# Output weights of an attention layer gated and split in an earlier stage, and the merge of its patterns begun two slots later

## The chip, the cores and the metric

The kernel runs on one core of one Trainium2 chip. The metric is the device time of the whole program in microseconds (us). Less is better. TensorE is called PE here, VectorE DVE, ScalarE ACT, GpSimd POOL, SyncE SP.

## The reference, cut to what matters

A trunk of two layers over a sequence of 1024 rows of 1024 features, in float32. Layer 0 mixes by a gated MLP (gMLP), layer 1 by dilated attention; each is followed by a squared-ReLU MLP of 4096 hidden features. Every sub-layer is modulated by a conditioning vector: `h = x * (1 + scale) + shift; x = LayerNorm(alpha * x + gate * f(h))`. The change concerns the attention of layer 1 and its output weights:

```python
def mixer_b(h, w_qkv, w_out, slopes):
    B, S, _ = h.shape
    qkv = (h @ w_qkv).reshape(B, S, N_PAT, 3, B_HEADS, B_HEAD_DIM)
    outs, lses = [], []
    for g, (window, dilation) in enumerate(B_PATTERNS):   # (128,1), (512,4), (2048,16)
        o, lse = dilated_branch(qkv[:, :, g, 0], qkv[:, :, g, 1], qkv[:, :, g, 2],
                                window, dilation, slopes)
        outs.append(o); lses.append(lse)
    wts = jax.nn.softmax(jnp.stack(lses, axis=0), axis=0)[..., None]
    o = jnp.sum(wts * jnp.stack(outs, axis=0), axis=0)
    return o.reshape(B, S, B_HEADS * B_HEAD_DIM).astype(h.dtype) @ w_out
```

There are 16 heads of 64, three patterns (dilation 1, 4 and 16), and a softmax over the patterns' log-sums merges their outputs. The gate, a row of 1024 numbers, multiplies the columns of `o @ w_out`; the kernel multiplies it into the columns of `w_out` instead.

## The kernel before

Float32 operands are split into a high and a low part (`hi` is a cast by ACT, `lo` is the remainder by DVE; lines L102 and L103 of a helper `split`), and each product is three matmuls: hi x hi, hi x lo, lo x hi. The MLPs and the projections of the attention go by a seven-product scheme on 2 x 2 blocks of 512.

In order of time the program is: layer 0's mixer and MLP; **the values stage** (function `values`); **the attention** (function `attention`), with the projection of q and k of the dilated patterns woven in; the output projection; the second MLP (`mlp(3, ...)`).

The values stage runs over `V_STEPS`, five sets of seven products `p`: v of pattern 2, of pattern 1, of pattern 0, then q and k of pattern 0 (the undilated one, `g == 0`). A product takes four steps `m`, each with 12 matmuls into `psv` (L1257). Weights are loaded raw (`vraw`, two products ahead, method `load` of `RightForms`), some into tiles of a tag `res` and others of other tags (helper `raw_tile`), and split one product ahead into `vrhi`, `vrlo`. `evict` combines, splits and stores results: v, q and k go to DRAM over POOL's queue.

The attention takes 24 groups, three patterns of each of eight pairs of heads `hp`; a group owns eight slots, and a slot has ordered lists of pieces of work, put there with `at(slot, half)`. A group's pieces are scores, a softmax pass (ACT and DVE), transposes, `halve` (tiles pT into `pThi`, `pTlo`), `weighted` (matmuls `pv<-pThi,v` and `pv<-pTlo,v`, L1527) and `gather` (ACT and DVE add the halves of `pv` into `oT`, L1536 and L1537). When a pair's three patterns are there, `merge(hp, oTs)` reads their log-sums, forms weights, writes them to `w_dram`, loads them spread over partitions into `bc` (L1611 and others) and does twelve steps on DVE: scale `oT` by `bc` (L1623), add (L1627), cut into high and low. For pairs 0 to 6 these steps are put at slots from `base + 9` on, where `base` is the first slot after the pair's last group; pair 7's are called by hand in `go_on`.

The output projection sums 8 units `k` (one pair of heads each, 128 rows of `w_out`) in five calls of `accumulate`: a (units 0 to 3, first half of the rows, tile `psoa`), b (0 and 1, second half, `psob`), c (2 and 3, `psoc`), d (4 to 7, first half, `psod`) and e (4 to 7, second half, `psoe`). a and b run inside the last groups' slots, c and d after them in `go_on`, and e is a callback at the entry of the second MLP. A unit's weights are made by `staged_unit`: the raw 512 KB load (L1708), the product with the gate row (L1712), and the split into `wo_hi` and `wo_lo`, each at a slot given relative to the last group. Raw tiles have the tag `raw` (2 buffers), hi and lo tiles the tags `whi` and `wlo` (4 buffers each). The tag `raw` also serves the raw weights `up` of the MLPs (L754).

Within each engine the order is the program's only where `keep_in_program_order` asks for it; elsewhere a scheduler orders by its own model. Each engine works its queue in order, and SP issues the loads in order, each once its tile is free.

Of the kernel before, what the change touches and what calls it, by code (L numbers as in the profile page):

```python
# [10 lines left out]
F32 = mybir.dt.float32  # L11
F32R = mybir.dt.float32r
AF = mybir.ActivationFunctionType
ALU = mybir.AluOpType
# [3 lines left out]
P = 128  # L18
S = 1024
D = 1024  # L20
NT = S // P
KD = D // P
HALF = 512
D_FF = 4096
N_HEADS = 16
N_PAIRS = N_HEADS // 2
# [9 lines left out]
def trunk(ctx: ExitStack, tc: tile.TileContext, x, c, ada_w, ada_b, ln_g, ln_b, a_w_in, a_b_in,  # L36
# [3 lines left out]
    nc = tc.nc  # L40
    V, A, G, T = nc.vector, nc.scalar, nc.gpsimd, nc.tensor

    def pool(stack, name, bufs, **kw):
        return stack.enter_context(tc.tile_pool(name=name, bufs=bufs, reuse_waits="tile", **kw))
# [5 lines left out]
    wts = pool(ctx, "wts", 4)  # L50
    work = pool(ctx, "work", 2)
    dram = pool(ctx, "dram", 1, space=DRAM)
# [44 lines left out]
    def bank(kind, name):  # L97
        return ps[kind].tile([P, HALF], F32, name=name, tag=kind)

    def split(hi, lo, src, hi_engine=A, lo_engine=V):  # L100

        first = A.copy(hi, src) if hi_engine is A else hi_engine.tensor_copy(hi, src)  # L102
        return first, lo_engine.tensor_tensor(lo, src, hi, op=ALU.subtract)  # L103
# [4 lines left out]
    gate_dram = dram.tile([4, D], F32, name="gate_dram")  # L108
# [93 lines left out]
    def run(gen):  # L202
        for _ in gen:
            pass
# [867 lines left out]
    v_dram = [dram.tile([S, N_PAIRS, 4 * HEAD], F32, name=f"v_{g}") for g in range(3)]  # L1072

    qk_dram = dram.tile([N_PAIRS, 2, P, 2, S], F32, name="qk_0")

    class RightForms:
        BLOCK = {1: (0, 0), 2: (1, 0), 5: (0, 1), 6: (1, 1), 7: (0, 1), 4: (1, 0)}
# [53 lines left out]
    def values(before, right, ahead):  # L1131
        run(ahead)
        form = before.form
        name = {1: "L11", 2: "L12", 5: "S1", 6: "S2", 7: "S3", 4: "L22", 3: "S4"}
        with ExitStack() as ph:
# [12 lines left out]
            def x_tile(nm):  # L1148
                return xp.tile([P, HALF], F32, name=nm, tag="x")
# [12 lines left out]
            def place(f, k, src):  # L1162
                split(form[f][:, 0, k, :], form[f][:, 1, k, :], src)
# [48 lines left out]
            stream = second()  # L1212
            sums, parts = {}, {}

            def evict(g, X, p, m):
                acc = sums["pb" if p in (2, 5, 3) else "pa", m][:]
                if p in (1, 5, 6):
                    t = parts[p, m] = x_tile(f"vpart_{g}_{X}_{p}_{m}")
                    A.copy(t[:], acc)
                    return  # L1220
                if p != 4:
                    t = parts.pop(({2: 1, 7: 5, 3: 6}[p], m))
                    V.tensor_tensor(t[:], acc, t[:], op=ALU.add)
                    acc = t[:]
                half, dh = {2: (1, 0), 3: (1, 1), 4: (0, 0), 7: (0, 1)}[p]
                if X < 2:
                    t = parted.tile([P, 2, HALF], F32R, name=f"qs_{X}_{p}_{m}", tag="vs")
                    split(t[:, 0], t[:, 1], acc)
                    nc.gpsimd.dma_start(qk_dram[4 * dh + m, X, :, :, half * HALF : (half + 1) * HALF], t[:].bitcast(F32))
                    return  # L1230
                v = parted.tile([P, 4, 4, HEAD], F32R, name=f"vs_{g}_{p}_{m}", tag="vs")
                split(v[:, :, 0:4:3, :], v[:, :, 1:3, :], acc.rearrange("p (h e c) -> p h e c", e=2, c=HEAD))
                i = 4 * half + m
                nc.gpsimd.dma_start(v_dram[g][i * P : (i + 1) * P, 4 * dh : 4 * dh + 4, :],
                                  v[:].rearrange("p h f c -> p h (f c)").bitcast(F32))

            for n, (g, X, p) in enumerate(V_STEPS):
                while name[p] not in built:
                    next(stream)
                for m in range(4):  # L1240
                    if m % 2 == 0 and n + 1 < len(V_STEPS):
                        right.prepare(*V_STEPS[n + 1], m // 2)
                    if m % 2 and n + 2 < len(V_STEPS):
                        right.load(*V_STEPS[n + 2], m // 2)
                    if p in (1, 2, 5):
                        kind = "pa" if p == 1 else "pbx" if m > 1 and n > 1 else "pb"
                        sums["pa" if p == 1 else "pb", m] = bank(kind, f"psv{p}_{g}_{X}_{m}")
                    acc = sums["pb" if p in (2, 5, 3) else "pa", m][:]
                    left = form[name[p]]
                    for kp in range(2):  # L1250
                        r = right.ready[g, X, p, kp]
                        for k in range(2):
                            for a, b in TERMS:
                                rows, cols_ = left[:, a, 2 * kp + k], r[b][:, k]
                                if X < 2:
                                    rows, cols_ = r[a][:, k], left[:, b, 2 * kp + k]
                                T.matmul(acc, rows[:, m * P : (m + 1) * P], cols_,  # L1257
                                         start=p in (1, 2, 5) and kp + k + a + b == 0,
                                         stop=kp == 1 and k == 1 and a == 1, skip_group_check=True)
                    evict(g, X, p, m)  # L1260
                    if n or m > 1:
                        next(stream, None)
                    if (g, X) == V_STEPS[-1][:2] and p == 6:
                        if m == 0:
                            form["L21"] = form["S1"]
                        place("L21", m, l21[m][:])
# [5 lines left out]
    def attention(form):  # L1272
# [5 lines left out]
        with ExitStack() as ph:  # L1278
            open_psum(ph, "B", sc=2, pv=2, mm=2, tr=2)
            ql = pool(ph, "attn_qlo", 1)  # L1280
            vec = pool(ph, "vecB", 1)
# [35 lines left out]
            ending = {}  # L1317
# [57 lines left out]
            def at(slot, pos, rank=4):  # L1375
                def put(f):
                    slots[slot][pos].append((rank, f))
                return put
# [190 lines left out]
            def merge(hp, oTs):  # L1569

                base = 8 * (3 * hp + 3)
                box = {}
# [67 lines left out]
                pieces = ((scale, 2), (scale, 1), (scale, 0), (add, 2), (add, 1), (cut, 0))  # L1640
# [3 lines left out]
                steps = [lambda f=f, g=g, half=half: f(g, half) for f, g in pieces for half in range(2)]  # L1644
                pace = 2 if hp < N_PAIRS - 2 else 1
                for n, f in enumerate(steps):
                    n = pace * n + 18
                    at(base + n // 2, n % 2)(f)

            for hp in range(N_PAIRS):  # L1650
# [37 lines left out]
            last_group = 8 * (len(order) - 1)  # L1688
# [1 line left out]
            ending["units"] = {}  # L1690
            done = ending["res"] = Residual(2)

            def pinned_split(hi, lo, src):
                for x_ in split(hi, lo, src):
                    tc.keep_in_program_order(x_)

            @at(last_group - 13, 0)
            def gate_row():
                ending["gate"] = vec.tile([P, D], F32, name="gate_2", tag="oT", bufs=4)
                nc.sync.dma_start(ending["gate"][:], gate_dram[2].partition_broadcast(P))  # L1700

            def staged_unit(k, load, gate, ready):
                box = {}

                @at(last_group + load[0], load[1])
                def load_raw():
                    box["raw"] = wts.tile([P, D], F32, name=f"wo_{k}_raw", tag="raw", bufs=2)
                    nc.sync.dma_start(box["raw"][:], b_w_out[0, k * P : (k + 1) * P, :])  # L1708

                @at(last_group + gate[0], gate[1])  # L1710
                def apply_gate():
                    tc.keep_in_program_order(V.tensor_tensor(box["raw"][:], box["raw"][:], ending["gate"][:], op=ALU.mult))  # L1712

                def split_raw():
                    hi, lo = (wts.tile([P, D], F32R, name=f"wo_{k}_{m}", tag=f"w{m}")[:] for m in ("hi", "lo"))
                    pinned_split(hi, lo, box["raw"][:])
                    ending["units"][k] = hi, lo

                if ready is None:
                    return split_raw  # L1720
                at(last_group + ready[0], ready[1])(split_raw)

            staged_unit(0, (-14, 0), (-12, 0), (-11, 0))
            staged_unit(1, (-13, 0), (-11, 1), (-10, 1))
            staged_unit(2, (-11, 0), (-10, 0), (-9, 0))
            staged_unit(3, (-10, 1), (-9, 1), (-8, 0))
            staged_unit(4, (-2, 0), (2, 0), (8, 0))
            staged_unit(5, (-1, 0), (4, 0), (8, 1))
            late = [staged_unit(6, (9, 0), (11, 1), None), staged_unit(7, (9, 1), (12, 1), None)]

            @at(last_group - 9, 0)
            def rows_first():
# [45 lines left out]
            def go_on():  # L1778
                steps = ending["merge"]
                for n, _ in enumerate(accumulate(1, range(2, 4), name="c")):  # L1780
                    if n > 4:
                        steps.pop(0)()
                for f in late:
                    f()
                for f in steps:
                    f()
                run(accumulate(0, ((4, 5, 6), (7,)), last=True, side=2, name="d"))
# [9 lines left out]
            stream = project()  # L1797
# [60 lines left out]
```

## Time and profile before

| | |
|---|---|
| device time, three runs | 2725.7, 2727.11, 2728.95 us; median 2727.11 |
| the profiled execution: time, span | 2727.96, 2726.2 us |
| mean granted clock of PE | 0.995 |
| values stage, pattern 0 | about 1225 to 1380 us of the span |
| attention, with a and b of the output projection | about 1377 to 2032 us |
| c, d and e of the output projection | 2032.8 to 2095.4 us |
| first product of the second MLP (`psua`) | from 2095.63 us |

In the lines shown below, a line of the busy windows gives a stretch of the span, its length, and for each engine its busy time and the number of instructions (x), then PE's granted clock as a share of full speed, the share of the 16 DMA engines that was busy, and GB/s. A line of a timeline gives start, length, engine, line of the kernel, operation, tiles and shape, and in brackets how long the engine sat idle before it and what ended that. A line of a tile's view gives minimum, median and maximum of one instruction's time in ns, and the first and last start. A line of the waits gives the total, the number of times and the longest, in us.

### The profile page before, as it was taken

The numbers are of one execution on the slowest core, as the hardware profiler recorded it, in microseconds if no ns is written. First come the engines' busy times: TensorE is split into PE (matmuls) and PEld (weight loads), VectorE is DVE, ScalarE is ACT, GpSimd is POOL, SyncE is SP. The second block draws the span as 40 slices with busy tenths as digits, with TensorE's granted clock in tenths as the row PEclk, the third lists the DMA queues.
The fourth block names the chain that finished last, engine by engine and source line by source line (L and its number), as shares of the span: only waits on it lengthen the run. The fifth ranks groups of instructions, "written<-read, shape, count | busy, mean of one in ns | idle before, by whom it ended". The sixth has DMA issues, their size and how long they took to land.

```text
span 2726.2 us, 36911 instructions
## 1 busy us (share of the span) xinstructions
PE 2658.8 (98%) x13242; PEld 2196.3 (81%) x13242; DVE 1989.8 (73%) x3594; ACT 1377.1 (51%) x2593; POOL 97.0 (4%) x161
## 2 busy tenths in 40 slices
PE   6999999999999999999999999999999999999998
PEld 5788888887888878888888888888777788878886
DVE  6787698787867778555557767777768966577877
ACT  3354375555443464434436666666655655554332
POOL 1000000000000000111110000000010000000000
PEclk9999999999999999999999999999999999999999
DMA  7534346667936545655565554555672654485562
GB/s 263 159 118 134 116 140 224 227 214 257 333 131 194 195 155 193 212 186 182 178 210 153 155 140 129 132 144 139 193 183 105 202 189 159 149 311 192 171 207 86
DMA packets 332572, 487.98 MB, mean 179 GB/s; under 512 B 50988, under 2 KB 176340, under 8 KB 332388
## 3 DMA queue, kind: packets, MB, share of 16 engines
q1 hardware_dynamic: 318564, 435.29, 50.3%
q0 software_dynamic: 13824, 50.34, 5.2%
q8 instruction: 104, 1.70, 0.3%
q14 instruction: 80, 0.66, 0.1%
HBM read 357.01 MB, written 128.53 MB: 178 GB/s over the span
## 4 chain that ended last, share of the span: by engine, by line
PE 77%; DVE 12%; DMA 6%; ACT 3%; issue 2%; SPq 1%; DVEq 0%; ACTq 0%
PE psd L955 22%; PE psv L1257 13%; PE psua L796 7%; PE psq L1358 6%; PE psk L1358 6%; DMA adaw<-in_ada_w_dram 3%; PE psuc L796 3%; PE psd_wout L389 3%; PE psu L368 3%; PE pv L1527 3%; PE sc L1447 2%; PE psv L470 2%; PE psub L796 2%; DVE adaacc L128 1%; DVE left L103 1%
## 5 line engine op out<-in xcount | busy, mean ns | idle before, releaser
L796 PE MATMUL psua<-right,left 128*128 128x512 f32 x1536 | 363.4, 390 | 0.3
L955 PE MATMUL psd<-rhi,lhi 128*128 128x512 f32 x896 | 349.9, 390 | 3.0 <-ACT part L827 3.0
L955 PE MATMUL psd<-rlo,lhi 128*128 128x512 f32 x896 | 349.6, 390 | 0.2
L955 PE MATMUL psd<-rhi,llo 128*128 128x512 f32 x896 | 349.2, 390 | 0.0
L796 PEld LDWEIGHTS psua<-right,left 128*128 128x128 f32 x1536 | 287.1, 188 | 61.7 <-DVE right L103 1.4
L1469 ACT ACTIVATE p<-p,stat 128x128 f32<-128x128 f32 (+1 forms) x384 | 168.7, 441 | 107.8 <-DVE stat L1467 104.7
L955 PEld LDWEIGHTS psd<-rhi,lhi 128*128 128x128 f32 x896 | 168.6, 188 | 39.1 <-ACT part L827 3.9
L955 PEld LDWEIGHTS psd<-rlo,lhi 128*128 128x128 f32 x896 | 168.5, 188 | 35.9 <-DVE rlo L103 1.1
L955 PEld LDWEIGHTS psd<-rhi,llo 128*128 128x128 f32 x896 | 168.6, 188 | 35.0
L796 PE MATMUL psuc<-right,left 128*128 128x512 f32 x768 | 187.2, 390 | 0.0
L128 DVE SCALAR_TENSOR_TENSOR adaacc<-adaw,silu_c,adaacc 128x512 f32<-128x512 f32 x168 | 128.5, 775 | 55.0 <-DMA adaw<-in_ada_w_dram 54.6
L796 PEld LDWEIGHTS psuc<-right,left 128*128 128x128 f32 x768 | 143.5, 188 | 30.0 <-DVE right L103 0.4
L103 DVE TENSOR_TENSOR pTlo<-pT,pThi 128x512 fp32r<-128x512 f32 (+1 forms) x160 | 99.3, 621 | 75.1 <-ACT pThi L102 74.1
L103 DVE TENSOR_TENSOR left<-ws,left 128x512 fp32r<-128x512 f32 x128 | 87.8, 688 | 71.5 <-ACT left L102 69.7
L103 DVE TENSOR_TENSOR llo<-lraw,lhi 128x1024 fp32r<-128x1024 f32 x112 | 136.4, 1218 | 0.8 <-ACT lhi L102 0.8
L102 ACT CAST left<-ws 128x512 fp32r<-128x512 f32 x128 | 79.1, 620 | 99.1 <-DVE ws L717 87.8
L1358 PE MATMUL psk<-form_L,wqk_hi 128*128 128x512 f32 x384 | 127.0, 412 | 0.0
L1358 PE MATMUL psq<-form_L,wqk_hi 128*128 128x512 f32 x384 | 126.4, 410 | 0.0
L102 ACT CAST rhi<-rraw 128x1024 fp32r<-128x1024 f32 x48 | 50.6, 1053 | 139.6 <-issue 113.7
L1257 PE MATMUL psv<-vrhi,form_S 128*128 128x512 f32 x384 | 119.9, 390 | 0.6 <-ACT vrhi L102 0.4
L102 ACT CAST lhi<-lraw 128x1024 fp32r<-128x1024 f32 x112 | 117.4, 1048 | 3.5 <-PE psua L796 3.5
L1467 DVE CUSTOM_DVE_ANT_0 p<-sc,bias 128x128 f32<-128x128 f32 (+1 forms) x384 | 113.6, 346 | 6.7 <-PE sc L1447 5.8
(326 smaller groups left out, 6094.4 us busy)
## 6 DMA issues: line engine op xcount, KB each, us to landing
lraw<-forms SPq DMA_DIRECT2D x112, 512.0 KB
adaw<-in_ada_w_dram SPq DMA_DIRECT2D x192, 256.0 KB
up<-in_mlp_w_up_dram SPq DMA_DIRECT2D x64, 512.0 KB
forms<-s SPq DMA_DIRECT2D x128, 256.0 KB
rraw<-in_mlp_w_down_dram SPq DMA_DIRECT2D x64, 512.0 KB
forms<-part SPq DMA_DIRECT2D x96, 256.0 KB
v<-vs POOLq DMA_DIRECT2D x48, 512.0 KB, 3.7
vraw<-in_b_w_qkv_dram SPq DMA_DIRECT2D x42, 512.0 KB
```

The source lines that it names most:

```text
L102: first = A.copy(hi, src) if hi_engine is A else hi_engine.tensor_copy(hi, src)
L103: return first, lo_engine.tensor_tensor(lo, src, hi, op=ALU.subtract)
L128: ins = V.scalar_tensor_tensor(acc[:], raw[:], silu_c[:, k : k + 1], acc[:], ALU.mult, ALU.add)
L368: T.matmul(dst, s[a], m[b], start=(n == 0), stop=(n == last))
L389: T.matmul(p[:], stat[a][:, k, o : o + P], u[b][:, w], start=n == 0, stop=n == count - 1)
L796: T.matmul(acc, w[:, a, k, :], right[p][:, b, k, :], start=p in (1, 2, 5) and k + a + b == 0, stop=k == 3 and a == 1, skip_group_check=True)
L955: ins = T.matmul(sums[kind, m][:], l[a][:, k, m * P : (m + 1) * P], r[b][:, k, :], start=p in (1, 5, 2, 3) and kp + k + a + b == 0, stop=k ...
L1257: T.matmul(acc, rows[:, m * P : (m + 1) * P], cols_, start=p in (1, 2, 5) and kp + k + a + b == 0, stop=kp == 1 and k == 1 and a == 1, ski ...
L1358: T.matmul(p[:], wu[a][:, k * P : (k + 1) * P], h_op(k, half, b), start=k + c_ == 0, stop=k == KD - 1 and c_ == 2)
L1467: V.tensor_tensor_reduce(out=pr, in0=banks[e][:, sl], in1=st["bias"][:, width - w :], scale=-0.125, scalar=3e38, op0=ALU.add, op1=ALU.min, ...
L1469: A.activation(pr, pr, AF.Exp, bias=nm, scale=-1.0, accum_out=l)
L1527: T.matmul(pvs[b][:, q0 % HALF : q0 % HALF + w_], stt, x_[:, o_ : o_ + w_], start=not begun[b], stop=left[b] == 0, skip_group_check=True)
```

## The change

The gate and split of the output weights move from the end of the attention to the values stage. During the 21 products of pattern 0, a 256 KB piece (one half of a unit's columns) is loaded into a tile of the tag `res` at `m == 2` of a product; at `m == 1` of the next, DVE multiplies it with the gate, ACT and DVE split it, and POOL's queue stores high and low parts (512 KB) to a new DRAM array `wo_parts`. There are sixteen pieces. The two halves of the gate row are loaded beforehand into two tiles of the tag `h`. At the end of the attention, `staged_unit` and the gate row's load go; `load_unit(k)` loads a unit's high and low parts from `wo_parts`, 512 KB each, with no arithmetic. Unit 6 takes the two `raw` tiles, the others `whi` and `wlo`. The merge's steps of pairs 0 to 6 begin at `base + 11`.

```diff
+    wo_dram = dram.tile([N_PAIRS, P, 2, 2, HALF], F32, name="wo_parts")
...
+            gate, pieces, begun = [], deque((k, dh) for k in range(N_PAIRS) for dh in range(2)), deque()
+
+            def gate_halves():
+                for dh in range(2):
+                    gate.append(work.tile([P, HALF], F32, name=f"gate_2_{dh}", tag="h"))
+                    nc.sync.dma_start(gate[dh][:], gate_dram[2, dh * HALF : (dh + 1) * HALF].partition_broadcast(P))
+
+            def piece_load():
+                k, dh = pieces.popleft()
+                t = work.tile([P, 2, HALF], F32R, name=f"wo_{k}_{dh}", tag="res", bufs=3)
+                nc.sync.dma_start(t[:, 1].bitcast(F32), b_w_out[0, k * P : (k + 1) * P, dh * HALF : (dh + 1) * HALF])
+                begun.append((k, dh, t))
+
+            def piece_store():
+                k, dh, t = begun.popleft()
+                raw = t[:, 1].bitcast(F32)
+                V.tensor_tensor(raw, raw, gate[dh][:], op=ALU.mult)
+                split(t[:, 0], t[:, 1], raw)
+                nc.gpsimd.dma_start(wo_dram[k, :, dh, :, :], t[:].bitcast(F32))
+
             for n, (g, X, p) in enumerate(V_STEPS):
+                if (g, X, p) == (1, 2, 3):
+                    run(stream)
+                    gate_halves()
...
                     evict(g, X, p, m)
+                    if g == 0 and m == 1 and begun:
+                        piece_store()
+                    if g == 0 and m == 2 and pieces:
+                        piece_load()
...
-                    n = pace * n + 18
+                    n = pace * n + 22
                     at(base + n // 2, n % 2)(f)
...
-            staged_unit(0, (-14, 0), (-12, 0), (-11, 0))
-            staged_unit(1, (-13, 0), (-11, 1), (-10, 1))
-            staged_unit(2, (-11, 0), (-10, 0), (-9, 0))
-            staged_unit(3, (-10, 1), (-9, 1), (-8, 0))
-            staged_unit(4, (-2, 0), (2, 0), (8, 0))
-            staged_unit(5, (-1, 0), (4, 0), (8, 1))
-            late = [staged_unit(6, (9, 0), (11, 1), None), staged_unit(7, (9, 1), (12, 1), None)]
+            def load_unit(k):
+                ending["units"][k] = tuple(wts.tile([P, D], F32R, name=f"wo_{k}_{m}", tag="raw" if k == 6 else f"w{m}", bufs=2 if k == 6 else 4)[:] for m in ("hi", "lo"))
+                for i, t in enumerate(ending["units"][k]):
+                    nc.sync.dma_start(t.rearrange("p (d c) -> p d c", c=HALF).bitcast(F32), wo_dram[k, :, :, i, :])
+
+            for k, slot in enumerate((-15, -14, -12, -9, 8, 9, 4)):
+                at(last_group + slot, 1)(lambda k=k: load_unit(k))
...
-                for f in late:
-                    f()
+                load_unit(7)
```

More of the change, by code (lines that the diff above doesn't have):

```diff
@@ L1691, in attention @@
             done = ending["res"] = Residual(2)
[L1693 to L1721, printed above, removed]
-            staged_unit(0, (-14, 0), (-12, 0), (-11, 0))
-            staged_unit(1, (-13, 0), (-11, 1), (-10, 1))
-            staged_unit(2, (-11, 0), (-10, 0), (-9, 0))
-            staged_unit(3, (-10, 1), (-9, 1), (-8, 0))
-            staged_unit(4, (-2, 0), (2, 0), (8, 0))
-            staged_unit(5, (-1, 0), (4, 0), (8, 1))
-            late = [staged_unit(6, (9, 0), (11, 1), None), staged_unit(7, (9, 1), (12, 1), None)]
+            def load_unit(k):
[4 more added lines that the diff above has]
+                at(last_group + slot, 1)(lambda k=k: load_unit(k))
             @at(last_group - 9, 0)
```

## The prediction

> **What bounds the kernel now.** I read the page first (busy shares, clock), then the busy windows by stage, then the timeline of TensorE (PE) wherever a window is not full.
>
> ```profile
> span 2726.2 us, 36911 instructions
> PE 2658.8 (98%) x13242; PEld 2196.3 (81%) x13242; DVE 1989.8 (73%) x3594; ACT 1377.1 (51%) x2593; POOL 97.0 (4%) x161
> ...
> core 0: us, PE busy (x) PEld busy (x) DVE busy (x) ACT busy (x) POOL busy (x), PEclk, DMA share, GB/s
> 1225.00:1300.00 75.00, 75.00 (x333) 62.10 (x332) 41.94 (x49) 30.81 (x43) 10.45 (x16) 1.00 0.55 193
> 1300.00:1380.00 80.00, 80.00 (x355) 66.24 (x354) 43.98 (x55) 34.02 (x48) 13.16 (x19) 1.00 0.55 192
> ...
> 1965.00:1970.00 5.00, 1.79 (x11) 1.65 (x12) 4.30 (x9) 2.78 (x8) 0.00 (x0) 0.93 0.97 370
> 1970.00:1975.00 5.00, 4.66 (x23) 3.38 (x21) 5.00 (x9) 3.54 (x8) 0.00 (x0) 0.73 0.50 149
> 1975.00:1980.00 5.00, 2.69 (x27) 2.15 (x25) 5.00 (x8) 1.06 (x2) 0.00 (x0) 0.95 1.01 340
> 1980.00:1985.00 5.00, 5.00 (x17) 4.12 (x18) 4.40 (x17) 3.51 (x14) 1.71 (x3) 0.71 1.08 368
> ...
> 2030.00:2035.00 5.00, 3.96 (x12) 3.19 (x13) 4.31 (x9) 1.52 (x3) 0.00 (x0) 0.57 0.91 254
> 2035.00:2040.00 5.00, 5.00 (x18) 4.01 (x17) 3.70 (x5) 0.00 (x0) 0.00 (x0) 0.74 0.51 125
> 2095.00:2100.00 5.00, 5.00 (x25) 4.15 (x24) 5.00 (x14) 3.11 (x5) 0.00 (x0) 1.00 0.20 80
> ```
>
> PE is busy 98% of the span, so moved work pays only where PE waits. In the stage that receives the work (the two rows 1225 to 1380) PE has no idle time; VectorE (DVE) is busy 85.9 of 155 us. The end of attention, which loses the work, is one of the few holes: DVE full for two rows, PE 1.79 and 2.69 of 5, and a granted clock of 0.71 to 0.73 after the idle. The timeline of PE there, idle before each instruction in brackets:
>
> ```profile
> 1957.48 0.33 PE L1447 MATMUL sc<-khi,qhi 64*128 64x128 f32 x2 [0.17 <-ACT khi L102]
> 1958.12 0.33 PE L1527 MATMUL pv<-pTlo,v 128*128 128x128 f32 x1 [0.32 <-DVE pTlo L103]
> 1967.71 0.33 PE L1527 MATMUL pv<-pThi,v 128*128 128x128 f32 x1 [3.26 <-ACT pThi L102]
> 1968.53 0.33 PE L1527 MATMUL pv<-pTlo,v 128*128 128x128 f32 x1 [0.49 <-DVE pTlo L103]
> 1971.49 0.80 PE L1756 MATMUL psoa<-wo_lo,oTs 128*128 128x512 f32 x1 [0.34 <-DVE wo_lo L103]
> 1978.22 0.33 PE L1527 MATMUL pv<-pTlo,v 128*128 128x128 f32 x1 [2.27 <-DVE pTlo L103]
> ...
> 2027.66 0.44 PE L1527 MATMUL pv<-pThi,v 128*128 128x256 f32 x2 [0.40 <-ACT pThi L102]
> 2028.39 0.39 PE L1527 MATMUL pv<-pTlo,v 128*128 128x256 f32 x1 [0.28 <-DVE pTlo L103]
> 2030.47 0.39 PE L1527 MATMUL pv<-pTlo,v 128*128 128x256 f32 x1 [0.95 <-DVE pTlo L103]
> 2032.07 0.58 PE L1527 MATMUL pv<-pTlo,v 128*128 128x256 f32 x1 [0.57 <-DVE pTlo L103]
> ...
> 2095.63 2.88 PE L796 MATMUL psua<-right,left 128*128 128x512 f32 x12
> ```
>
> Place A, 1955 to 1985: 0.17 + 0.32 + 3.26 + 0.49 + 0.34 + 2.27 = 6.85 us idle. Clock lost, as busy time x (1 - clock): 0.13 + 1.26 + 0.13 + 1.45 = 3.0. Place B, 2027 to 2040: 0.40 + 0.28 + 0.95 + 0.57 = 2.20 idle, and 1.70 + 1.30 = 3.0 of clock. Together 15.0 us can be had there.
>
> **Removed at the end of attention.**
>
> ```profile
> L1712 DVE TENSOR_TENSOR wo_raw<-wo_raw,gate x8: 1205/1218/1226, 1952.7 to 2036.2; 128x1024 f32<-128x1024 f32 x8
> L102 ACT CAST wo_hi<-wo_raw x8: 1044/1048/1058, 1953.9 to 2046.5; 128x1024 fp32r<-128x1024 f32 x8
> L103 DVE TENSOR_TENSOR wo_lo<-wo_raw,wo_hi x8: 1203/1216/1225, 1955.0 to 2049.8; 128x1024 fp32r<-128x1024 f32 x8
> ...
> 1963.92 1.98 DVE L1623 TENSOR_TENSOR bc<-oT,bc 128x512 f32<-128x512 f32 x2 [1.97 <-DMA bc<-w_dram]
> ...
> DVE bc L1623 <- DMA bc<-w_dram: 8.5, 3, 3.7
> PE pv L1527 <- DVE pTlo L103: 2.7, 4, 1.2
> PE pv L1527 <- ACT pThi L102: 0.3, 1, 0.3
> ```
>
> Eight units leave 8 x (1.218 + 1.216) = 19.5 us of DVE and 8 x 1.048 = 8.4 of ScalarE (ACT) between 1952.7 and 2051. The 2.27 and 0.34 of place A end on DVE while it works through units and merge, so both shrink. The 3.26 is another matter: the merge's scaling (bc, L1623) stands at the head of DVE's queue and waits 1.97 us for its loads; oT, pT and PE follow it in turn. The merge two slots (some 6.4 us) later meets loads that have landed: the longest such wait in the attention window 1500 to 1700 (the last three rows are its waits) is 3.7. In that static order the next head's gathers and pT splits come first.
>
> Against it: unit 3 now comes as two 512 KB loads in place of one, on queues that are full (DMA share 0.97 to 1.08), issued behind the merge's loads, and PE wants it about 1965. I let 2.85 of the 9.85 stay for that and for the short waits on ACT: A gains 7 (3 to 9.85). At B the two splits at 2028 to 2031 go, but the last head's chain of softmax, transpose and split, which has no cover, stays: I take half, 2.5 of 5.2 (0.5 to 5.2). In mid-attention the same shift of the merge removes at most the PE waits of the three rows, 2.7 + 0.3: 3.0 (1 to 3.0). The eight merges' own work is unchanged.
>
> On the clock, a rule of the Trainium skill (TensorE: Matmul & The Clock Gate, "Part 1: The HAM clock gate") says that half clock follows only after an idle window of some 3.4 us. This trace differs: 2.27 us idle was followed by 0.71. By the rule A and B would return idle time alone; the sum goes by the rows.
>
> **Added in the values stage.** Sixteen pieces of 128x512, one in each of the first 16 of 21 products of the undilated pattern. The nearest rows are the MLP's weights of that shape:
>
> ```profile
> L102 ACT CAST left<-up x96: 602/617/630, 351.5 to 2392.7; 128x512 fp32r<-128x512 f32 x96
> L103 DVE TENSOR_TENSOR left<-up,left x96: 671/685/693, 352.1 to 2394.0; 128x512 fp32r<-128x512 f32 x96
> L754 SPq DMA_DIRECT2D up<-in_mlp_w_up_dram x64: 367/383/2135, 304.9 to 2354.0; - x64
> ...
> v<-vs POOLq DMA_DIRECT2D x48, 512.0 KB, 3.7
> ```
>
> DVE: 16 x 2 x 0.685 = 21.9 us; ACT: 16 x 0.617 = 9.9. With 85.9 of 155 busy DVE goes to 70%, so throughput suffices. SP issues 16 loads and two gate halves at 0.38, 7 us more in a stage where weights are fetched far ahead. DMA: 16 loads of 256 KB and 16 stores of 512 KB, 12 MB beside the 30 MB of 155 us at 193 GB/s; the share goes from 0.55 to about 0.77. POOL's queue takes 16 stores between those of v, q and k; behind them wait only further stores. What covers all this is that PE's next weights lie ready; I take 0 (0 to 5). It may not be below 0: PE is full there.
>
> The later loads (16 x 512 KB in place of eight and the 512 KB gate row) are covered but for unit 3 above and unit 7, issued when c has freed its tiles (about 2046) and wanted about 2054: 8 us for 1 MB. I take 0 (0 to 3).
>
> **Moved without being named: the first weights of the last MLP.** Unit 6 now lies in the two tiles of the "raw" ring. In before that ring is free early and the up weights come in one group:
>
> ```profile
> 2049.89 6.02 SPq L754 DMA_DIRECT2D up<-in_mlp_w_up_dram  x5
> ...
> 228.52 4.08 DMA wout_raw<-in_a_w_out_dram
> 999.19 5.56 DMA v_r<-in_b_w_qkv_dram
> 2403.46 4.27 DMA heldt<-in_mlp_w_down_dram
> ```
>
> In the changed order up_3_0_0 and up_3_1_0 take the tiles of unit 6 and wait on SP until PE's last read of it, three matmuls before the end of e. PE goes straight from there to psua_3_0, which needs up_3_0_0 loaded and cast. Three matmuls are 3 x 0.24 = 0.7 (12 in 2.88). The stall: 4.2 for 512 KB (4.08, 4.27; 5.56 the worst row) + 0.62 cast + 0.5 (my allowance for issue and signals) - 0.7 = 4.6 us. Behind the waiting load on SP stand spills, forms and adaLN loads; behind left_3_0_1 on ACT and DVE the rest of the entry. Nothing gives it back: 2095 to 2100 is full of PE. After such idles the clock lost 1.26 (place A, after 3.26), 1.45 (after 2.27) and 3.0 (B); their mean is 1.9. Cost: 6.5 (4.3 with the 4.08 row, less allowance and no dip, to 6.0 + 3.0 = 9.0 with the 5.56 row).
>
> **Sum.** -7 - 2.5 - 3 + 6.5 + 0 = -6.0. The profiled run took 2727.96 (span 2726.2 and 1.76 around it), 0.85 above the median of 2727.11; so 2722.0 against that run and 2721.1 against the median.
>
> **Rivals.**
>
> *A: the entry of the MLP is nearly free.* If the two loads land faster on an idle queue (share 0.20 at 2095) and no dip follows, the entry costs 2.5 us in place of 6.5: -12.5 + 2.5 = -10, or 2717; with all gains at their ends and an entry of 4.3, -18.05 + 4.3 = -13.8, 2713. Against it: no 512 KB row is under 3.7.
>
> *B: the ring stalls the values stage (slower).* Three "res" tiles now serve pieces as well as weights. A piece holds one through its load, three quarters of a 7.4 us product (155/21), 2.0 of split and a 3.7 store, some 11 us in 7.4: half of the ring's three tiles. If weights then come one store late (3.7) and the clock dips by 1.45, each such product costs 5.2. One takes the gain away to -0.8; from three on it is slower: -6 + 15.6 = +9.6, 2737. For it: PE has no slack there, and 512 KB have taken 5.56 (v_r) where queues were full. Against: 69 us of idle DVE, and weights fetched many products ahead. Apart from the rows, the Trainium skill (SBUF, "SBUF: two separate sides") warns that POOL-issued transfers starve while DVE holds the shared port, 620 ns becoming about 3100; by that estimate sixteen stores would each take 2.5 us more. The v stores, beside a DVE as busy, took 3.7, which neither shows nor excludes it.
>
> *C: the holes at the end refill.* Queues are full at A; if unit 3 and the gathers land 3 us late and the dips stay, A gives 3, B 0.5, middle 2: -5.5 + 6.5 = +1.0, 2728.
>
> **How the numbers follow.** 0.2% (5.45 us) is about what a measurement of this kernel tells from no change: faster is below 2721.7, slower above 2732.6. Forecast 0.42, of which 0.26 lies below 2721.7 and 0.16 above; A 0.17; C 0.16; B 0.25, counted as slower whole (two late products and C's small gains would do as well as three). Faster 0.43, same 0.32, slower 0.25. The forecast's own range is 2717 to 2725; that for 8 in 10 reaches from A's lower end, 2713, to B's three products, 2737.
>
> **What would show it.** Right: PE full from 1955 to 1985 with a clock near 1.00; no DVE wait on bc there; two up loads issued near the last psoe and an idle of PE of 4 to 5.5 us before the first psua, with a dip behind it; 1225 to 1380 still full. Wrong: idle PE in the values stage on vraw's splits (B); psoa waiting for loads (C); the first psua within 2.5 us of the last psoe (A).

## The result, and the profile after

The changed kernel is slower: 2741.15 us median of seven runs against 2728.95 of before in the same comparison, ratio 1.0045 with a 95% interval of 1.003 to 1.006. The forecast was 2721, and 2713 to 2737 was its range for 8 in 10. The span grew from 2726.2 to 2739.3, by 13.1 us.

Where they went is read from four marks on PE: the transpose that ends the wait on `h` before the values stage, the last matmul of that stage, the first `psoc`, and the last `psoe`. The second line of each fence is one kind of matmul of the values stage; its last start lies 10.9 us ahead of the stage's last matmul in both kernels.

```profile
971.50 1.32 PE L221 MATMUL pst<-ident,acc 128*128 128x128 f32 x8 [0.71 <-ACT h L226]
L1257 PE MATMUL psv<-form_L,vrlo x48: 389/389/389, 1301.3 to 1365.9; 128*128 128x512 f32 x48
L1756 PE MATMUL psoc<-wo_hi,oTs x32: 389/389/735, 2032.8 to 2045.7; 128*128 128x512 f32 x32
```

```profile
967.71 1.32 PE L221 MATMUL pst<-ident,acc 128*128 128x128 f32 x8 [0.71 <-ACT h L226]
L1281 PE MATMUL psv<-form_L,vrlo x55: 388/389/504, 1300.1 to 1381.9; 128*128 128x512 f32 x55
L1754 PE MATMUL psoc<-wo_hi,oTs x32: 388/389/441, 2039.6 to 2050.3; 128*128 128x512 f32 x32
L1754 PE MATMUL psoe<-wo_hi,oTs x64: 387/389/499, 2075.8 to 2102.0; 128*128 128x512 f32 x64
```

(The first fence is before, whose last `psoe` starts at 2095.4, the second is after.) The stages in us, from such marks, for every kernel that was run:

| kernel | start | values | attention to c | c to e | rest | span |
|---|---|---|---|---|---|---|
| before | 971.5 | 405.3 | 656.0 | 62.6 | 630.8 | 2726.2 |
| after | 967.7 | 425.1 | 646.8 | 62.4 | 637.3 | 2739.3 |
| e1_no_arith | 969.0 | 418.6 | 649.7 | 60.6 | 634.2 | 2732.1 |
| e2_store_other | 970.7 | 416.3 | 645.0 | 62.2 | 637.4 | 2731.5 |
| e3_unit6 | 973.1 | 426.9 | 645.1 | 62.6 | 629.3 | 2736.9 |
| e4_shift_only | 973.0 | 406.1 | 657.3 | 62.9 | 630.0 | 2729.3 |
| e5_no_shift | 971.4 | 426.6 | 647.1 | 62.4 | 634.4 | 2741.9 |
| e6_x | 974.3 | 408.1 | 646.3 | 62.1 | 636.7 | 2727.5 |
| e7_x_unit6 | 972.0 | 407.5 | 646.8 | 62.3 | 630.4 | 2719.0 |
| e8_unit3_raw | 974.5 | 405.9 | 642.6 | 62.2 | 629.4 | 2714.6 |
| e9_unit3_no_shift | 969.3 | 408.0 | 642.8 | 62.2 | 629.4 | 2711.7 |

The start varies by 7 us between kernels although nothing differs ahead of it; that is the scatter of a single execution. After against before: start -3.8, values +19.8, attention -9.2, c to e -0.2, the MLP's entry and what follows +6.5; the sum is +13.1.

The values stage, which had no idle PE, now has it. First the busy windows of before and after (the last two rows are after, behind its two longest waits), then the timeline of PE in after, then waits in after on PE, DVE and SP (total us, times, longest):

```profile
1150.00:1400.00 250.00, 250.00 (x1105) 207.01 (x1104) 137.54 (x162) 102.24 (x142) 34.52 (x56) 1.00 0.59 199
...
1150.00:1400.00 250.00, 239.09 (x1026) 194.78 (x1025) 150.10 (x185) 102.56 (x148) 41.02 (x67) 0.98 0.66 229
...
1211.00:1219.00 8.00, 7.81 (x27) 6.28 (x28) 5.05 (x8) 3.94 (x6) 1.59 (x3) 0.79 0.69 216
1258.00:1270.00 12.00, 11.90 (x41) 9.60 (x42) 9.30 (x12) 5.94 (x9) 3.30 (x5) 0.76 0.62 228
```

```profile
1199.67 0.50 PE L1281 MATMUL psv<-vrhi,form_S 128*128 128x512 f32 x1 [1.01 <-ACT vpart L1220]
1211.19 0.50 PE L1281 MATMUL psv<-vrhi,form_L 128*128 128x512 f32 x1 [2.98 <-DVE vpart L1224]
1232.50 0.50 PE L1281 MATMUL psv<-form_L,vrlo 128*128 128x512 f32 x1 [1.25 <-DVE vrlo L103]
1258.10 1.19 PE L1281 MATMUL psv<-form_S,vrhi 128*128 128x512 f32 x2 [5.34 <-DVE vpart L1224]
...
PE psv L1281 <- DVE vpart L1224: 8.6, 3, 5.3
...
DVE wo L1254 <- DMA wo<-in_b_w_out_dram: 35.9, 10, 7.5
...
SPq L1248 <- DMA wo_parts<-wo: 47.2, 10, 8.4
SPq L1100 <- DMA wo_parts<-wo: 32.0, 5, 10.9
```

Of the 19.8 us, 10.9 are idle time of PE (250 less 239.09). Another 4.5 are clock: 7.81 x 0.21 and 11.90 x 0.24 in the two rows behind the long waits. A dip to 0.73 from 971 to 976, ahead of any piece, is 1.4 more, and no other run has it. About 3 us are not accounted for.

One turn of it, from the timelines of POOL, SP and DVE in after:

```profile
1200.58 0.54 POOL L1256 DMA_DIRECT2D wo_parts<-wo  x1 [9.41 <-DVE wo L103]
1205.29 0.34 SPq L1248 DMA_DIRECT2D wo<-in_b_w_out_dram  x1
1209.84 0.69 DVE L1254 TENSOR_TENSOR wo<-wo,gate 128x512 f32<-128x512 f32 x1 [4.06 <-DMA wo<-in_b_w_out_dram]
1210.45 0.68 DVE L1224 TENSOR_TENSOR vpart<-psv,vpart 128x512 f32<-128x512 f32 x1
...
1254.39 0.69 DVE L1254 TENSOR_TENSOR wo<-wo,gate 128x512 f32<-128x512 f32 x1 [5.71 <-DMA wo<-in_b_w_out_dram]
1257.27 0.68 DVE L1224 TENSOR_TENSOR vpart<-psv,vpart 128x512 f32<-128x512 f32 x1
```

A piece is stored at 1200.58. The next piece's load waits on SP until that store has landed and goes at 1205.29. Its multiplication stands at the head of DVE's queue and waits 4.06 us for it. Behind it, in the same queue, stands the eviction that frees a PSUM bank; it runs at 1210.45 and PE goes on at 1211.19, 2.98 late. The longest wait of PE, 5.34 us at 1258.10, came the same way: the last two lines are a piece's multiplication that waited 5.71 us and the eviction behind it, with two other instructions between them. The raw weights of the stage wait for such stores too (L1100, 32.0 us in five).

The two other places that the forecast named, in after:

```profile
1981.81 0.80 PE L1754 MATMUL psoa<-wo_hi,oTs 128*128 128x512 f32 x1 [3.02 <-DMA wo_hi<-wo_parts]
...
2101.48 0.93 SPq L754 DMA_DIRECT2D up<-in_mlp_w_up_dram  x2
2106.86 1.22 PE L796 MATMUL psua<-right,left 128*128 128x512 f32 x2 [4.51 <-ACT left L102]
...
1980.00:1985.00 5.00, 3.19 (x10) 2.23 (x11) 1.62 (x9) 1.09 (x4) 0.00 (x0) 0.56 1.05 403
1985.00:1990.00 5.00, 5.00 (x23) 4.17 (x22) 1.78 (x2) 2.38 (x7) 0.91 (x1) 0.76 1.07 389
2025.00:2040.00 15.00, 13.61 (x87) 11.33 (x86) 9.44 (x25) 9.43 (x20) 2.08 (x3) 1.00 0.81 177
2105.00:2110.00 5.00, 3.13 (x7) 2.51 (x8) 2.67 (x7) 2.78 (x4) 0.00 (x0) 0.69 0.62 210
```

At place A of the prediction one wait of 3.02, on unit 3's loads, stands in place of the 6.85, with a dip behind it (0.56, then 0.76). At place B 1.4 us of idle are left and no dip. At the MLP's entry the two up loads go at 2101.48 and PE stands 4.51 us, with a dip to 0.69.

### The profile page after: what moved, and what is told of

It reads as the page before. It is cut to its first block, busy times and chain, and to the rows that moved or that the text cites. A ratio compares the mean times of both kernels' runs of the same rounds, so it can differ in the third digit from the quotient of the medians.

```text
span 2739.3 us, 37039 instructions
## 1 busy us (share of the span) xinstructions
PE 2664.6 (97%) x13242; PEld 2198.5 (80%) x13242; DVE 1993.1 (73%) x3610; ACT 1377.8 (50%) x2601; POOL 105.9 (4%) x177
## 4 chain that ended last, share of the span: by engine, by line
PE 69%; DVE 11%; issue 10%; DMA 6%; ACT 3%; POOL 1%; SPq 1%; DVEq 0%; POOLq 0%; ACTq 0%
PE psd L955 22%; PE psua L796 8%; PE psq L1386 6%; PE psk L1386 6%; PE psuc L796 4%; PE psd_wout L389 3%; PE psu L368 3%; DMA adaw<-in_ada_w_dram 3%; PE pv L1555 3%; PE psv L1281 3%; PE sc L1475 3%; PE psv L470 2%; PE psub L796 2%; PE pT L1528 1%; DVE adaacc L128 1%
```

## The experiments

Theory 1: the ring of three `res` tiles, in which a piece sits until its store has landed, makes loads late, and DVE's in-order queue hands that on to PE. Theory 2: the added 12 MB are too much for the transfer queues. Theory 3: DVE has too much work.

**e1_no_arith.**

```diff
-                V.tensor_tensor(raw, raw, gate[dh][:], op=ALU.mult)
-                split(t[:, 0], t[:, 1], raw)
...
                 nc.sync.dma_start(t[:, 1].bitcast(F32), b_w_out[0, k * P : (k + 1) * P, dh * HALF : (dh + 1) * HALF])
+                nc.sync.dma_start(t[:, 0].bitcast(F32), b_w_out[0, k * P : (k + 1) * P, dh * HALF : (dh + 1) * HALF])
```

> Leaves out the gate's multiplication and the split of the sixteen pieces (each piece's two halves are loaded raw, 256 KB each, and stored as before), so the values stage has the changed kernel's transfers and 4 MB more, and none of its added VectorE and ScalarE work. Theory 1 (the piece's multiplication stands in VectorE's queue ahead of the evictions of PSUM and waits for a load that the ring of three tiles lets go late): TensorE's waits on vpart, 9.6 us in the changed kernel, fall to below 1.5 us, and the time to about 2726 (2741 less 10.8 idle and 5 of clock). Theory 2 (12 MB more on the transfer queues delay the weights and the stores of v, q and k): the stage still loses 10 us or more, 2741 or above. Theory 3 (VectorE has too much work): as theory 1.

Measured: 2734.48 us, ratio to before 1.0014 (1.0002 to 1.0025). The values stage takes 418.6, still 13.3 above before. PE's waits on `vpart` did fall, from 8.6 to 2.2, though not below the 1.5 expected; what remains is mostly late weights:

```profile
PE psv L1280 <- DVE vrlo L103: 6.7, 3, 4.0
PE psv L1280 <- DVE vpart L1224: 2.2, 4, 1.0
...
SPq L1100 <- DMA wo_parts<-wo: 38.2, 10, 6.0
SPq L1100 <- DMA wo<-in_b_w_out_dram: 23.8, 9, 6.9
```

The loads of weights (L1100) wait for pieces that are still being stored or loaded. So the in-order wait on DVE is one way from the ring to PE, and late weights are a second, which is rival B of the prediction. Theory 3 can't account for these 13.3 us: no work of DVE was added. The expected 2726 was missed. Theories 1 and 2 are not yet told apart.

**e2_store_other.**

```diff
-                nc.gpsimd.dma_start(wo_dram[k, :, dh, :, :], t[:].bitcast(F32))
+                nc.gpsimd.dma_start(wo_dram[k, :, dh, :, :], form["S4"][:, :, 0, :].bitcast(F32))
```

> The pieces are loaded, gated and split as in the changed kernel, but the 512 KB that POOL's queue stores at that point come from another resident tile (a factor form of the stage), so the output weights are other data and a piece's tile is free once its split is done, some 4 us earlier. Theory 1 with the store's landing as what holds the tile: VectorE's waits on the pieces' loads, 35.5 us in nine, fall below 12, TensorE's waits in the stage from 10.8 to below 3, time about 2728. Theory 1 with another hold (the raw weights that share the ring): they stay above 20, time about 2739. Theory 2: unchanged, 2741, as the same bytes go the same ways. Theory 3: unchanged, 2741, as VectorE has the same work.

Measured: 2732.8 us, 1.0014 (1.0001 to 1.0026). The expectation missed one thing: with nothing to wait for, all sixteen stores were issued early, between 1036 and 1078, beside the stores of v of other patterns. The windows of e2, then the first of them in before, then DVE's waits on the pieces' loads in e2:

```profile
1040.00:1110.00 70.00, 62.18 (x263) 49.71 (x262) 44.65 (x54) 24.86 (x36) 17.08 (x27) 0.98 0.82 302
1150.00:1400.00 250.00, 250.00 (x1104) 207.09 (x1103) 162.63 (x200) 109.57 (x158) 36.48 (x59) 1.00 0.62 214
...
1040.00:1110.00 70.00, 69.56 (x307) 57.16 (x306) 50.66 (x60) 31.26 (x45) 8.52 (x16) 1.00 0.67 230
...
DVE wo L1254 <- DMA wo<-in_b_w_out_dram: 22.1, 11, 6.0
```

Where the pieces are loaded, gated and split, PE is full again, with DVE at 162.63 of 250 us, more than in the changed kernel. That again speaks against theory 3, and for the store's landing as what makes the ring costly. But DVE's waits on the pieces' loads fell only from 35.9 to 22.1 us, not below 12 as expected, and none of what is left reached PE: their sum is not what PE pays. Where the stores are bunched, at 302 GB/s, PE is idle 7.8 us, against 0.4 in before, so PE's waits in the stage did not fall below 3 and the time not to 2728. A heap of stores can thus hold up PE, but the changed kernel has none; whether the 16 engines or POOL's queue, which the stores of v share, is the limit there was not tested.

**e6_x.** Same arithmetic, same bytes, other tiles: high and low each in one of nine tiles of tag `x`, mostly idle by then.

```diff
-                t = work.tile([P, 2, HALF], F32R, name=f"wo_{k}_{dh}", tag="res", bufs=3)
+                t, hi = (x_tile(f"wo_{k}_{dh}_{i}") for i in range(2))
...
-                nc.gpsimd.dma_start(wo_dram[k, :, dh, :, :], t[:].bitcast(F32))
+                for i, part in enumerate((hi, t)):
+                    nc.gpsimd.dma_start(wo_dram[k, :, dh, i, :], part[:])
```

> The changed kernel with the pieces in two tiles each of the nine of tag x, mostly idle by then, instead of the ring that the raw weights use; same bytes, same arithmetic, and a store of 256 KB for high and one for low. Ring theory: no load of weights waits for a piece's store, TensorE's waits in the values stage fall from 10.8 (8.9 without arithmetic) to below 1.5 us, the clock holds, 2741 less 15 is about 2726. Transfer theory: they stay at 8 us or more, 2738 or above.

Measured: 2725.98 us, 0.9985 (0.9976 to 0.9994), as the ring theory had it.

```profile
1150.00:1400.00 250.00, 248.55 (x1092) 204.15 (x1091) 159.46 (x197) 108.32 (x156) 52.80 (x89) 1.00 0.72 246
...
PE psv L1281 <- DVE vpart L1224: 1.5, 4, 0.6
...
SPq L1248 <- DMA wo_parts<-wo: 10.1, 2, 6.3
...
DVE wo L1253 <- DMA wo<-in_b_w_out_dram: 21.7, 7, 6.6
```

No weight load waits for a piece's store any more, and PE's waits on `vpart` are 1.5, with some tenths of others. DVE still waits 21.7 us for the pieces' loads, up to 6.6 at once, and no wait of PE is over 0.7: what such a wait costs depends on what stands behind it and when that is needed. The transfer share is 0.72, above the 0.66 of the changed kernel that stalled. Theory 2 falls for this stage. The stage takes 408.1, 2.8 above before; the same stage takes 405.9 to 408.0 in e7 to e9.

**e3_unit6.**

```diff
-tag="raw" if k == 6 else f"w{m}", bufs=2 if k == 6 else 4
+tag=f"w{m}", bufs=4
...
+                load_unit(6)
                 load_unit(7)
...
-                run(accumulate(0, ((4, 5, 6), (7,)), last=True, side=2, name="d"))
+                run(accumulate(0, ((4, 5), (6, 7)), last=True, side=2, name="d"))
```

> Unit 6's weights go to the rings of the other units, loaded after c with unit 7, and the d sums take units 4 and 5, then 6 and 7; the two raw tiles are free for the MLP's first weights, as in the kernel before. If the wait at the MLP's entry comes from those tiles: the two up loads are issued by 2060 instead of 2101, the 4.5 us of idle before the first psua and the dip after it go, 2741 less 6 is about 2735. Rival: the wait only moves, units 6 and 7 land 3 to 5 us after d wants them: 2739 to 2741.

Measured: 2737.63 us, 1.0027 (1.0015 to 1.0039). From the last `psoe` to the end takes 629.3 instead of 637.3, c to e 62.6 instead of 62.4, and the first `psua` follows 0.2 us after the last `psoe`. The up loads go at 2065.38, not by 2060 as expected, but early enough. The two tiles of unit 6 are the cause, and the time from c to e shows no wait that moved to d.

**e4_shift_only** and **e5_no_shift** take the merge's shift apart from the rest: `pace * n + 18` becomes `+ 22` in the kernel before, and `+ 22` becomes `+ 18` in the changed one.

> The kernel before with nothing but the merge's start two slots later. If the 3.26 us wait at 1967 and those in mid-attention come from the merge waiting for bc at the head of VectorE's queue: TensorE's waits on pT fall by 5 to 6 us and the clock loss by 1.3, 2729 less 6 is about 2723. If the units' arithmetic at the end is what counts, the shift gives 3 at most: 2726 or above.

> The changed kernel with the merge's start put back to base + 9. If shift and lighter VectorE are worth something only together (the shift alone gave nothing, its 3.26 us came back as waits on the units' splits): the wait on pThi of about 3 us at the end of attention returns, and first psq to first psoc, 646.6 us in the changed kernel, goes back to about 651; 2741 + 4 = 2745. If the units' removal alone makes the gain: 646.6 stays, 2741.

Measured: 2729.21 us, 0.9997 (0.9986 to 1.0008), for the shift alone, and 2741.66 us, 1.0043 (1.0026 to 1.0059), for the change without it. PE in e4, at the two places:

```profile
1970.84 0.80 PE L1756 MATMUL psoa<-wo_lo,oTs 128*128 128x512 f32 x1 [3.57 <-DVE wo_lo L103]
2031.30 0.55 PE L1527 MATMUL pv<-pThi,v 128*128 128x256 f32 x2 [2.56 <-ACT pThi L102]
```

The 3.26 us wait went, and 3.57 and 2.56 came: DVE had the same work to do in the same time. In mid-attention (1500 to 1700), where the kernel before waits 2.7 and 0.3 us on pT, the shift did help; the first two lines are e4, the others the changed kernel:

```profile
PE pv L1527 <- ACT pThi L102: 0.6, 1, 0.6
PE pv L1527 <- DVE pTlo L103: 0.5, 1, 0.5
...
PE pv L1555 <- DVE pTlo L103: 0.7, 2, 0.5
PE pv L1555 <- ACT pThi L102: 0.6, 1, 0.6
```

So 1.9 of the 3.0 us went, and the end of attention gave them back. On the whole time the interval allows the shift -3.8 to +2.2 us. In e5, without the shift, DVE still waits for the merge's loads, and more than with it:

```profile
DVE bc L1651 <- DMA bc<-w_dram: 24.1, 8, 5.0
...
DVE bc L1651 <- DMA bc<-w_dram: 9.8, 2, 5.0
```

(The first line is e5, the second the changed kernel, both from 1500 to 2080.) PE's stage is 647.1 with 24.1 us of such waits and 646.8 with 9.8. Once DVE has room, they hardly reach PE: its waits on pT from 1500 to 1700 are 2.2 in e5 and 1.3 in the changed kernel, and the wait on pThi of about 3 us at the end did not come back.

**e7_x_unit6** joins e6 and e3.

> The pieces in tiles of tag x, and unit 6 in the rings of the other units, loaded after c. If the two costs are apart and add: 2741 less 15 less 6.5 is about 2719.5, faster than the kernel before (2729) by 6 to 9 us. If either comes back elsewhere: 2726 or above.

Measured: 2719.14 us, 0.9963 (0.9951 to 0.9976). Values 407.5, rest 630.4: the two costs are apart, and they add. What remains is the wait for unit 3, and the dip behind it:

```profile
1969.50 0.72 PE L1754 MATMUL psoa<-wo_hi,oTs 128*128 128x512 f32 x1 [2.87 <-DMA wo_hi<-wo_parts]
...
1970.00:1975.00 5.00, 5.00 (x20) 3.92 (x20) 3.43 (x10) 2.66 (x10) 0.00 (x0) 0.70 1.05 408
```

**e8_unit3_raw** and **e9_unit3_no_shift**, on top of e6:

```diff
-            for k, slot in enumerate((-15, -14, -12, -9, 8, 9, 4)):
+            for k, slot in ((0, -15), (1, -14), (3, -13), (2, -12), (6, 4), (4, 8), (5, 9)):
...
-tag="raw" if k == 6 else f"w{m}", bufs=2 if k == 6 else 4
+tag="raw" if k == 3 else f"w{m}", bufs=2 if k == 3 else 4
```

> Pieces in tiles of tag x as in e6; unit 3 goes to the raw tiles (free again after c, long before the MLP's weights want them) and is loaded two slots before unit 2, and unit 6 takes the fourth pair of the other rings, loaded well ahead of d; d is grouped as in the changed kernel. Against e7 (2719): the 2.9 us of waiting for wo_hi at the first sums of units 2 and 3 and the dip behind it (clock 0.70, 1.5 us) should go, and so should some of the 1.0 and 1.7 us waits in d: 2715. If the queues of that moment are the limit and not the order, the wait stays or moves to another load: 2719.

> As e8, with the merge's start put back to base + 9. If the shift is worth nothing once VectorE is relieved: the same time as e8 within 2 us. If it is worth something where nothing else waits: 2 to 4 us more than e8.

Measured: 2715.26 us, 0.9944 (0.9931 to 0.9956), and 2716.51 us, 0.9944 (0.993 to 0.9957). The wait on `wo_hi` is gone in both, attention takes 642.6 and 642.8, and no effect of the shift is seen. The other part of the expectation missed: in e8, waits of 1.5 us in d and 1.2 in e stand where e7 has 1.7 and 1.0 in d. These are the fastest versions, 0.56% below before.

## Why the prediction was wrong

**The values stage, taken at 0 (0 to 5), cost 19.8.** This step failed, and alone it turns the forecast round. The prediction asked whether DVE, ACT, SP and the queues had the throughput for the pieces, and they have (e6). It took the stage as covered because PE's next weights lie ready, and held that behind the pieces' stores on POOL's queue wait only further stores. In the changed kernel the next loads into the ring wait for those stores to land: 47.2 us of waits on SP for pieces, 32.0 for weights. It did not ask, of the one added instruction that waits for a load, what stands behind it: the evictions of PSUM, and behind those PE, which had no slack. That is the question that it put to the merge's scaling and not to the piece's multiplication.

**Rival B had the place and half the mechanism.** It saw that the ring would be shared, but followed only the weights (e1: a real way, 6.7 us), not DVE's queue (8.6 us in the changed kernel). It also put 21 products into 155 us, 7.4 each. The rows from 1225 to 1380 are only q and k, 14 of the 21; the stage's 405 us hold 35 products, 11.6 each, and the pieces started at 1115. With 11.6 in place of 7.4, B's own count is 8.7 + 2.0 + 3.7, some 14 us in 11.6: four tenths of the ring's three tiles, not half. The loads came late all the same, because a tile comes free in the order of the ring: ten of the sixteen pieces' loads waited for an earlier piece's store, in the turn shown for the one right before it. How the 19.8 divide between the two ways was not measured apart, since the runs that take one away change the order of the other. POOL's stores were no slower than those of v: both landed in 4.2 us by the median in the changed kernel, not in the 6.2 that 2.5 us more would give.

**Attention: -12.5 forecast, -9.2 measured.** No term came at its size; that the first two together were forecast at 9.5 is chance. Place A gave 4.2 of 9.85, not 7: of the 2.85 us that were to stay for unit 3 and short waits on ACT, unit 3 alone took 3.02 of idle and 2.6 of clock (3.19 x 0.44 and 5.00 x 0.24). Place B gave 3.8 of 5.2, not 2.5. Mid-attention gave 1.7, not 3.0. The merge's shift was wrong in mechanism at A: the 3.26 was put down to a wait on `bc` at the head of DVE's queue, but the shift alone only moved it (e4), and without the shift the units' removal gives the same attention time (e5, 647.1). The wait was named by what ended it; what lay behind it was that DVE had no room.

**The MLP's entry: +6.5 forecast, +6.5 measured**, with 4.51 of idle against 4.6. Mechanism and place were right; e3 and e7 remove it. That the size agrees to a tenth is luck: e3 against the changed kernel gives 8.0, e7 against e6 6.3, and the dip in the row shown is 1.0 (3.13 x 0.31), not the 1.9 of the sum.

**The clock.** Dips came again, of 1.0 to 2.9 us where the sum took 1.9: 0.56 after 3.02 us, 0.69 after 4.51, 0.76 after 5.34. The Trainium skill's rule (TensorE: Matmul & The Clock Gate, "Part 1: The HAM clock gate") of some 3.4 us of idle does not fit the first of these.

## What to carry to other kernels

When work is moved into a stage whose bound engine has no idle time, count its waits before its microseconds: for each added instruction that waits for a load, name what stands behind it in its queue, and for each tile that it borrows, who had that ring before and when the last reader (often a store) lets go. The sum of an engine's waits does not price them: e6 kept 21.7 us of them, and PE paid 1.5. A wait that a trace attributes to one load may only be the place where a full engine shows; test whether moving it does anything before giving it a term in a sum. A tile that is idle where it is borrowed may be the first that the next stage needs.

## What the runs showed of the hardware that was not expected

Sixteen stores of 512 KB issued within 42 us beside others (302 GB/s and a share of 0.82 in e2) came with 7.8 us of idle on a PE that was all but full there in before, while the same bytes spread over the stage (246 GB/s, 0.72, in e6) came with 1.5. In e7, 2.87 us of idle were followed by five at a granted clock of 0.70, which is 1.5 us more: a short stall cost half as much again as its idle time. Not every one does: in e2 an idle of 2.47 us that ended at 1103.83 was followed by a clock of 1.00, while in before 2.27 us were followed by 0.71:

```profile
1104.00:1108.00 4.00, 4.00 (x18) 3.28 (x18) 4.00 (x6) 1.96 (x3) 0.53 (x1) 1.00 0.32 129
```

What decides it is not shown here.
